# A transformer block on one core: x loaded a second time by tokens for its sums, warm-up matmuls, one power per norm, another order of projections

## The chip, the core and the metric

The kernel runs on one core of a Trainium2 chip. The metric is the device time of one execution in microseconds (us), lower is better. The engines named here are PE (the matrix engine, TensorE), PEld (its weight loads), DVE (VectorE), ACT (ScalarE), POOL (GpSimd) and SP, whose queue issues most transfers. Each engine runs its own instructions in the order in which the program holds them.

## What is computed

One block of a transformer on 512 tokens of width 1024 in fp32, cut here to its outline. Two attention mixers read the same normalized input, are gated and merged; a SwiGLU layer and a gated projection of a second input `p` follow.

```python
proj = rms_norm(x, g_mix) @ w_in                   # 1024 -> all heads, k, v, gates
q_n, kc_n, vc_n, ks_n, vs_n, kw_n, vw_n, gate_n, q_m, k_m, v_m, gate_a, gate_b = split(proj)
y_nsa  = nsa_mixer(...)    # 8 heads: compressed + selected + window attention, gated per head
y_moba = moba_mixer(...)   # 8 heads, causal, blocks of 256
x = x + (sigmoid(gate_a) * (y_nsa @ w_up_nsa) + sigmoid(gate_b) * (y_moba @ w_up_moba)) @ w_out
gate, up = split(rms_norm(x, g_ffn) @ w_ffn_in)    # 1024 -> 2 * 2816
x = x + (silu(gate) * up) @ w_ffn_out
x = x + sigmoid(rms_norm(x, g_ple) @ w_ple_gate) * (p @ w_ple_proj)
```

Queries and keys go through a norm over each head of 64 and a rotation of their first 16 elements (`partial_rope`) before the scores.

## The kernel before, in words

**Split numbers.** Every fp32 matrix is held as a high part (`wh`, `xh`) and a rest (`wl`, `xl`), and each product is three matmuls: high by high, high by rest, rest by high. A weight unit (128x1024, 512 KB) is loaded into one of three raw tiles `wr` on SP, copied to `wh` by ACT (line 83) and subtracted to `wl` by DVE (line 84). `Weights.units` lists the units in the order in which they are used; a unit is split about two units ahead of its matmuls, and each engine takes these copies in its own order among everything else.

**Start.** x comes transposed as eight tiles `xin` of 128x512. For each, ACT makes `xh` (line 220) and DVE `xl`; ACT squares it and POOL adds the squares up in `ssum` (lines 227 to 231). When the last is in, `rms_stats` sums `ssum` over partitions with four tiny matmuls into `st0b` (line 299) for the scales 1/rms of the 512 tokens; four more (`st0c`) spread the scales along rows.

**Projections.** `natural` multiplies a projection by four units of weights into four PSUM banks; the order is qm, km, qn (queries and keys of the two mixers), kT and vT with `compress_in` (inputs of the compressed keys and values), one gate tile, then cb and cc woven with the hidden layers of the compression (`khid`, `vhid`), then vm. `head_norm` squares on ACT, sums on DVE, takes the power -1/2 on POOL (line 356) for each 128-token tile, multiplies on DVE, rotates on POOL (lines 373 to 376) and splits on ACT and DVE (377, 378). `turned` transposes the result on PE into `QM`, `KM`, `QN`, `KN`.

**Attention.** 24 jobs, each of scores `sb` (711, 712), masks on DVE (714), exponentials on ACT (716), transposes `pt` of the probabilities (739), their split `pw` on ACT and DVE (748, 749) and products `pv` with the values. `weave` puts steps of other work between: `fill` (gate tiles `ga` and the projection `um`) at `FILL_RATE` steps per attention step, and `cmp_scores` at `CMP_RATE`. A scheduler then fixes each engine's order; the excerpts below are that order.

**Rest.** `un`, `wo`, the SwiGLU layer (`fi`, `fo`) and `pj`, `pg` follow, dense matmuls with weights streamed in.

Of the kernel before, what the change touches and what calls it, by code (L numbers as in the profile page):

```python
# [10 lines left out]
F32 = mybir.dt.float32  # L11
# [18 lines left out]
EARLY = 1  # L30
BIG_BUFS = 36
FILL_RATE = 0.83
CMP_RATE = 0.16
# [118 lines left out]
def hybrid_kernel(ctx: ExitStack, tc: tile.TileContext, a, out):  # L152
# [79 lines left out]

    for kt in range(KT):
# [62 lines left out]
    def rms_stats(name, tags="ss"):  # L296
        b = bank(name + "b", tags[0])
        for i in range(QT):
            T.matmul(b[:, i:i + 1], ssum[:, i * 128:(i + 1) * 128], ones[:, 0:1], start=True, stop=True)
        ms = small("ms_", [128, QT])  # L300
        V.tensor_scalar(ms, b[:, :QT], 1.0 / D, EPS, op0=OP.mult, op1=OP.add)
# [43 lines left out]
    def head_norm(items, nh, np_, gain, es, tables=None):  # L345
        n = nh * DH
        p = slice(0, np_)
        v3 = lambda t: t.rearrange("p (h d) -> p h d", d=DH)
        es = [e[p, :n] for e in es]
        for e, (src, ti, rn, r2, dst) in zip(es, items):  # L350
            A.activation(e, src, AF.Square)
            ss = small("ss_", [128, 8], bufs=4)
            V.tensor_reduce(ss[p, :nh], v3(e), axis=AX.X, op=OP.add)
            V.tensor_scalar(ss[p, :nh], ss[p, :nh], r2, EPS, op0=OP.mult, op1=OP.add)
            f = small("hf_", [128, 8], bufs=4)
            G.tensor_tensor(f[p, :nh], ss[p, :nh], half_neg[p, :nh], op=OP.pow)
            if rn is not None:
                V.tensor_scalar(f[p, :nh], f[p, :nh], rn, None, op0=OP.mult)
            V.tensor_tensor(v3(e), v3(src), f[p, :nh].unsqueeze(2).to_broadcast([np_, nh, DH]), op=OP.mult)

        def turn_and_split(k):
            e, (src, ti, rn, r2, dst) = es[k], items[k]
            e3 = v3(e)
            if gain is not None:
                V.tensor_tensor(e3, e3, gain[p].unsqueeze(1).to_broadcast([np_, nh, DH]), op=OP.mult)
            ct, st = tables or (cs2, sn2)
            w = t2("rope")[p]
            ra = w[:, 0:nh * 16].rearrange("p (h d) -> p h d", d=16)
            rc = w[:, 128:128 + nh * 16].rearrange("p (h d) -> p h d", d=16)
            cs = ct[p, ti].unsqueeze(1).to_broadcast([np_, nh, 16])  # L370
            s1 = st[p, ti, 0:8].unsqueeze(1).to_broadcast([np_, nh, 8])
            s2 = st[p, ti, 8:16].unsqueeze(1).to_broadcast([np_, nh, 8])
            G.tensor_tensor(ra, e3[:, :, 0:16], cs, op=OP.mult)
            G.tensor_tensor(rc[:, :, 0:8], e3[:, :, 8:16], s1, op=OP.mult)
            G.tensor_tensor(rc[:, :, 8:16], e3[:, :, 0:8], s2, op=OP.mult)
            G.tensor_tensor(e3[:, :, 0:16], ra, rc, op=OP.add)
            A.activation(dst[:, :, 0:DH], e3, AF.Copy)
            V.tensor_sub(dst[:, :, DH:128], e3, dst[:, :, 0:DH].bitcast(F32))

        return [lambda k=k: turn_and_split(k) for k in range(len(items))]  # L380
# [47 lines left out]
    def heads(sts, dst, tags, eng):  # L428
        for n in range(8):
            turned(sts, 2 * (n % 4), n // 4, tags[n % len(tags)], dst.tile(n % 4), eng)  # L430
            yield
# [8 lines left out]
    rb0, rn0, rhn0 = rms_stats("st0")  # L440
# [579 lines left out]
```

## Time and profile before

| what | value |
|---|---|
| time, median of 3 runs (all three) | 867.39 us (867.09, 867.39, 870.36) |
| the profiled execution | 869.85 us, its span 868.1 us |
| PE busy | 848.3 us, 98% of the span |
| DVE, ACT, POOL busy | 539.5, 388.2, 162.5 us |
| mean granted clock of TensorE | 0.991 |

The span runs from the first to the last instruction; the profiled execution has 1.75 us outside it. PE counts as busy from the start of a matmul to its modelled end, also when it runs at the lower clock, so 98% is not 98% of its peak. The granted clock is 1 at 2.4 GHz and 0.5 at 1.2 GHz.

### The profile page before, as it was taken

What the parts mean: (1) busy time and instruction counts of PE and PEld (TensorE: products, weight loads), DVE (VectorE), ACT (ScalarE), POOL (GpSimd) and SP (SyncE); (2) the same over time, 40 slices, a digit from 0 to 9 for tenths busy, and PEclk for the clock granted to TensorE, in tenths of its full rate; (3) what the DMA queues carried; (4) which work ended last, traced back from release to release, by engine and by line L of the source; (5) the groups of instructions that cost most, each with busy time, mean ns of one, the idle gap of its engine ahead of it and who ended that gap; (6) DMA issues with size and microseconds to landing.
All of it is one profiled execution on the core that took longest, in us unless ns stands there. A gap on an engine that the chain in (4) does not pass through costs nothing.

```text
span 868.1 us, 11091 instructions
## 1 busy us (share of the span) xinstructions
PE 848.3 (98%) x4157; PEld 710.9 (82%) x4157; DVE 539.5 (62%) x995; ACT 388.2 (45%) x702; POOL 162.5 (19%) x205
## 2 busy tenths in 40 slices
PE   7999999999999999999999999999999999999997
PEld 5787799788888888877888888888888888888886
DVE  7648967678997777749637555555555423333354
ACT  6344275677786677744433333333333223223421
POOL 6728914300000000006322111111111101010100
PEclk9999999999999999999999999999999999999999
DMA  7331365312311112115323223232323233333321
GB/s 249 102 98 61 90 186 183 99 49 73 98 49 50 52 48 70 33 67 189 124 75 97 98 97 97 98 98 97 97 97 97 85 94 106 91 109 97 97 97 48
DMA packets 26420, 83.49 MB, mean 96 GB/s; under 512 B 3328, under 2 KB 3840, under 8 KB 26368
## 3 DMA queue, kind: packets, MB, share of 16 engines
q1 hardware_dynamic: 25440, 80.69, 29.1%
q10 hardware_dynamic: 928, 2.11, 1.0%
q8 instruction: 32, 0.52, 0.2%
q14 instruction: 20, 0.16, 0.1%
HBM read 77.54 MB, written 2.10 MB: 92 GB/s over the span
## 4 chain that ended last, share of the span: by engine, by line
PE 86%; DVE 6%; POOL 3%; ACT 2%; issue 1%; DMA 1%; SPq 0%; ACTq 0%; POOLq 0%; DVEq 0%
PE fg L335 5%; PE fg L337 5%; PE fu L337 5%; PE fob L336 5%; PE fg L336 5%; PE fu L336 5%; PE fob L337 5%; PE fob L335 5%; PE fu L335 5%; PE ga L335 3%; PE ga L336 3%; PE ga L337 3%; PE pt L739 3%; PE pv L763 2%; PE pgb L335 2%; PE pgb L337 2%
## 5 line engine op out<-in xcount | busy, mean ns | idle before, releaser
L83 ACT ACTIVATE wh<-wr 128x1024 fp32r<-128x1024 f32 (+2 forms) x145 | 147.2, 1018 | 308.6 <-PE fu L336 69.8
L84 DVE TENSOR_TENSOR wl<-wr,wh 128x1024 fp32r<-128x1024 f32 (+2 forms) x145 | 195.2, 1348 | 112.9 <-ACT wh L83 111.6
L335 PE MATMUL fg<-x2h,wh 128*128 128x512 f32 x176 | 68.6, 390 | 0.0
L335 PE MATMUL fu<-x2h,wh 128*128 128x512 f32 x176 | 68.6, 390 | 0.0
L337 PE MATMUL fg<-x2h,wl 128*128 128x512 f32 x176 | 68.5, 389 | 0.0
L336 PE MATMUL fu<-x2l,wh 128*128 128x512 f32 x176 | 68.5, 389 | 0.0
L335 PE MATMUL fob<-HH,wh 128*128 128x512 f32 x176 | 68.5, 389 | 0.0
L336 PE MATMUL fg<-x2l,wh 128*128 128x512 f32 x176 | 68.5, 389 | 0.0
L337 PE MATMUL fob<-HH,wl 128*128 128x512 f32 x176 | 68.5, 389 | 0.0
L336 PE MATMUL fob<-HL,wh 128*128 128x512 f32 x176 | 68.5, 389 | 0.0
L337 PE MATMUL fu<-x2h,wl 128*128 128x512 f32 x176 | 68.5, 389 | 0.0
L908 POOL TENSOR_TENSOR u<-zg,u 128x512 f32<-128x512 f32 x22 | 29.9, 1360 | 199.7 <-DVE u L906 191.2
L231 POOL TENSOR_TENSOR ssum<-ssum,sqx 128x512 f32<-128x512 f32 x21 | 32.5, 1547 | 146.4 <-ACT sqx L230 146.3
L335 PE MATMUL ga<-xh,wh 128*128 128x512 f32 x128 | 53.5, 418 | 0.0
L714 DVE CUSTOM_DVE_ANT_0 p<-sb,big_mask 128x512 f32<-128x512 f32 (+2 forms) x96 | 44.4, 483 | 14.0 <-PE sb L712 13.8
L337 PE MATMUL ga<-xh,wl 128*128 128x512 f32 x128 | 51.2, 400 | 0.0
L336 PE MATMUL ga<-xl,wh 128*128 128x512 f32 x128 | 51.0, 398 | 0.0
L906 DVE SCALAR_TENSOR_TENSOR u<-fu,rb 128x512 f32<-128x512 f32 x22 | 15.2, 690 | 53.6 <-PE fu L337 53.6
L844 POOL TENSOR_TENSOR GT<-GT,GT 128x512 f32<-128x512 f32 x8 | 14.7, 1862 | 177.2 <-DVE GT L843 175.9
L336 PEld LDWEIGHTS fu<-x2l,wh 128*128 128x128 f32 x176 | 33.1, 188 | 6.9
L335 PEld LDWEIGHTS fob<-HH,wh 128*128 128x128 f32 x176 | 33.0, 188 | 6.9
L335 PEld LDWEIGHTS fg<-x2h,wh 128*128 128x128 f32 x176 | 33.1, 188 | 6.8
(640 smaller groups left out, 2028.3 us busy)
## 6 DMA issues: line engine op xcount, KB each, us to landing
wr<-fi SPq DMA_DIRECT2D x44, 512.0 KB, 3.3
wr<-ga SPq DMA_DIRECT2D x16, 512.0 KB, 3.5
wr<-fo SPq DMA_DIRECT2D x16, 512.0 KB, 3.5
wr<-wo SPq DMA_DIRECT2D x8, 512.0 KB, 3.4
wr<-pg SPq DMA_DIRECT2D x8, 512.0 KB, 3.3
wr<-fo SPq DMA_DIRECT2D x8, 384.0 KB, 3.1
xin<-xT SPq DMA_DIRECT2D x8, 256.0 KB, 5.8
wr<-km SPq DMA_DIRECT2D x4, 512.0 KB, 4.0
```

The source lines that it names most:

```text
L83: self.nc.scalar.activation(h[:, a:b], t[:, a:b], AF.Copy)
L84: self.nc.vector.tensor_sub(l[:, a:b], t[:, a:b], h[:, a:b].bitcast(F32))
L231: G.tensor_tensor(ssum, ssum, q, op=OP.add)
L335: T.matmul(o, wh[:, sl], h, start=start, stop=False)
L336: T.matmul(o, wh[:, sl], l, start=False, stop=False)
L337: T.matmul(o, wl[:, sl], h, start=False, stop=stop)
L714: V.tensor_tensor_reduce(out=p, in0=o, in1=big_mask[:, 512 - n:512], op0=OP.add, op1=OP.min, scale=1.0, scalar=3.0e38, accum_out=st["m"][: ...
L739: last = T.transpose(b[:, off:off + 128], st["p"][:, P_OFF[qt] + kb * 128:P_OFF[qt] + kb * 128 + 128], ident)
L763: T.matmul(o, job["v"](kb), st.pop(("pl", kb))[:, cols], start=False, stop=job["last"] and kb == 2)
L844: G.tensor_tensor(ta, ta, tb, op=OP.add)
L906: V.scalar_tensor_tensor(u, bu, 2.0, rb1, op0=OP.mult, op1=OP.mult)
L908: G.tensor_tensor(u, zg, u, op=OP.mult)
```

## The change

- The eight `xin` transfers stand ahead of everything else but the first weights; x comes a second time by tokens (`xN`, four tiles of 512 KB), and ACT squares these with a sum along each row (`sq`), in place of the squares, POOL's additions and the `st0b` matmuls.
- Eight fp32 matmuls of 128x128 on a tile of ones stand on PE ahead of the first real one.
- `head_norm` takes the power of all four tiles (128x32) in one POOL instruction, and sums, gains and rotations go by two tiles.
- kT and vT come right behind qm; `qn`'s transposes move behind cb; vm moves to just ahead of the attention; four steps of `fill`, the first score step and four more steps of `fill` come ahead of the weave; the compressed keys' chain (`cmp_kv`), `k_put` of cc and `cmp_scores` all run inside the attention at 0.28 steps per step; `FILL_RATE` 0.83 becomes 0.85.
- PSUM tags (`a`, `b`, `s`, `v`) are exchanged between cb, cc, khid, vhid and vm; `gsig` goes.

```diff
-FILL_RATE = 0.83
-CMP_RATE = 0.16
+WARM = 8
+FILL_RATE = 0.85
+CMP_RATE = 0.28
...
-    units = [*mixed("qm"), *mixed("km"), *mixed("qn")]
+    units = [*mixed("qm")]
     units += [(("kvc", i), a["kvc"][i], 1024) for i in range(2)]
+    units += [*mixed("km"), *mixed("qn")]
...
+    wb = bank("warm", "v")
+    for _ in range(WARM):
+        T.matmul(wb[:, 0:128], ones, ones, start=True, stop=True)
     for kt in range(KT):
         nc.sync.dma_start(xin[kt], a["xT"][kt])
-        if kt == 0:
-            W.load(1)
-        if kt % 2 == 1:
-            W.load(kt // 2 + 2)
+        if kt in (0, 3, 5):
+            W.load(W.n_raw + 1)
+    for kt in range(KT):
         norm_split(xin[kt], gv[:, 0, kt:kt + 1], xh[kt], xl[kt])
         if kt == 0:
             W.split(1)
-        add_square(xin[kt], kt == 0)
+    for tt in range(QT):
+        nc.sync.dma_start(flat(xn[tt]), a["xN"][tt])
+        A.activation(flat(xn[tt]), flat(xn[tt]), AF.Square, accum_out=sq[:, tt:tt + 1])
...
-        for e, (src, ti, rn, r2, dst) in zip(es, items):
-            A.activation(e, src, AF.Square)
-            V.tensor_reduce(ss[p, :nh], v3(e), axis=AX.X, op=OP.add)
-            G.tensor_tensor(f[p, :nh], ss[p, :nh], half_neg[p, :nh], op=OP.pow)
+        for g in groups:
+            for i in range(k, k + m):
+                A.activation(es[i], srcs[i], AF.Square)
+            V.tensor_reduce(ss[:, k * nh:(k + m) * nh], g[p].rearrange(...), axis=AX.X, op=OP.add)
+        G.tensor_tensor(f, ss, half_neg[p, :w], op=OP.pow)
...
-    cb_b = four("cb", "ab")
-    nat, hk = natural("cb", 256, cb_b), hidden("k", "s")
+    cb_b = four("cb", "sv")
+    nat, hk = natural("cb", 256, cb_b), hidden("k", "a")
...
-    side = k_put(kv_chunk(cb_b, 0, hg[:, 2]), 0, "b")
-    cc_b = four("cc", "vs")
-    nat, hv = natural("cc", 280, cc_b), hidden("v", "a")
+    side = chain(k_put(kv_chunk(cb_b, 0, hg[:, 2]), 0, "s"), heads(qn_t, QN, "s", "a"))
+    cc_b = four("cc", "ba")
+    nat, hv = natural("cc", 280, cc_b), hidden("v", "v")
...
-    cmp_side = cmp_scores()
-    fill = chain(gates(8 + EARLY, 16), up("um", YM, up_moba_done), gates(0, 8))
-    run(weave(weave(attention(jobs), fill, FILL_RATE), delay(cmp_side, 4), CMP_RATE))
+    vm_b = four("vm", "sv")
+    att = attention(jobs)
...
+    cmp_side = chain(cmp_kv(0, "k", "v"), cmp_kv(1, "v", "v"), side, cmp_scores())
+    fill = chain(gates(8 + EARLY, 16), gates(0, 2), up("um", YM, up_moba_done), gates(2, 8))
+    steps(fill, 4)
+    steps(att, 1)
+    steps(fill, 4)
+    run(weave(weave(att, fill, FILL_RATE), delay(cmp_side, 4), CMP_RATE))
```

**ACT's first work.** Behind two small loads ACT begins so before (`xh_86` is made from the first two tiles of x, `wh_90` from the first unit of weights, which comes in two halves):

```order
L227 ACTIVATE ssum<-xin_81 128x512
L220 ACTIVATE xh_86<-xin_81,gv 128x512
L83 ACTIVATE wh_90<-wr_83 128x512 x2
L220 ACTIVATE xh_86<-xin_81,gv 128x512
L230 ACTIVATE sqx<-xin_81 128x512
L83 ACTIVATE wh_190<-wr_98 128x1024
```

and so in the changed kernel, where `wh_115` is the first unit and `xh_111` the first two tiles:

```order
L84 ACTIVATE wh_115<-wr_94 128x512 x2
L223 ACTIVATE xh_111<-xin_92,gv 128x512 x2
L223 ACTIVATE xh_123<-xin_98,gv 128x512 x2
L84 ACTIVATE wh_186<-wr_101 128x1024
L223 ACTIVATE xh_129<-xin_103,gv 128x512
```

The first `xh` stood ahead of both halves of the first weights, and stands behind both now. PE's first real matmul needs it.

**PE where the attention starts.** Before, right behind the last matmuls of vm:

```order
L711 MATMUL sb<-KM_882,QM_528 128x512
L712 MATMUL sb<-k2M_1072,QM_528 128x512
L711 MATMUL sb<-KM_882,QM_528 128x384
L712 MATMUL sb<-k2M_1072,QM_528 128x384
L596 MATMUL kcT<-identr,MI 128x64
L392 MATMUL tb<-identr,kst 128x128 x4
L711 MATMUL sb<-KM_882,QM_528 128x256
L712 MATMUL sb<-k2M_1072,QM_528 128x256
L711 MATMUL sb<-KM_882,QM_528 128x128
L712 MATMUL sb<-k2M_1072,QM_528 128x128
L392 MATMUL tb<-identr,kst 128x128 x4
L711 MATMUL sb<-KM_882,QM_528 128x512
```

and in the changed kernel, behind eleven matmuls of the gate tile `ga` that follow vm:

```order
L733 MATMUL sb<-KM_899,QM_565 128x512
L734 MATMUL sb<-k2M_987,QM_565 128x512
L346 MATMUL ga<-xh_129,wh_1621 128x512
L347 MATMUL ga<-xl_130,wh_1621 128x512
L348 MATMUL ga<-xh_129,wl_1622 128x512
...
L348 MATMUL ga<-xh_135,wl_1622 128x512
L733 MATMUL sb<-KM_899,QM_565 128x384
L734 MATMUL sb<-k2M_987,QM_565 128x384
L733 MATMUL sb<-KM_899,QM_565 128x256
L734 MATMUL sb<-k2M_987,QM_565 128x256
L346 MATMUL ga<-xh_111,wh_1668 128x512
```

The transposes `tb` of the last keys left this place, and twelve gate matmuls stand between the first scores.

**PE where the attention ends.** Before, the transposes and products of the last two jobs have nine `uno` matmuls (the projection `un`) ahead of them and between:

```order
L763 MATMUL pv<-pw,VN_1080 128x512
L758 MATMUL pv<-pw,VN_1080 128x384
L335 MATMUL uno<-YNh_3134,wh_4145 128x512
...
L337 MATMUL uno<-YNh_3847,wl_4146 128x512
L763 MATMUL pv<-pw,VN_1080 128x384
L758 MATMUL pv<-pw,VN_1080 128x128
L763 MATMUL pv<-pw,VN_1080 128x128
L758 MATMUL pv<-phl,VN_1080 128x256
L763 MATMUL pv<-phl,VN_1080 128x256
L739 MATMUL pt<-ident,p 128x128 x8
L758 MATMUL pv<-pw,VN_1081 128x512
```

and in the changed kernel the last two jobs' transposes and products stand alone:

```order
L785 MATMUL pv<-phl,VN_996 128x256
L761 MATMUL pt<-ident,p 128x128 x4
L780 MATMUL pv<-pw,VN_995 128x512
L761 MATMUL pt<-ident,p 128x128 x2
L785 MATMUL pv<-pw,VN_995 128x512
L780 MATMUL pv<-pw,VN_995 128x384
...
L785 MATMUL pv<-phl,VN_995 128x256
L761 MATMUL pt<-ident,p 128x128 x4
L780 MATMUL pv<-pw,VN_996 128x512
L761 MATMUL pt<-ident,p 128x128 x2
L785 MATMUL pv<-pw,VN_996 128x512
```

Gate tiles and `uno` matmuls that stood here are used up some jobs earlier; one job more runs without other work between.

## Rows read from the trace of the kernel before

**Rows 1.** The page: each engine's busy time, share of the span, instructions.

```profile
PE 848.3 (98%) x4157; PEld 710.9 (82%) x4157; DVE 539.5 (62%) x995; ACT 388.2 (45%) x702; POOL 162.5 (19%) x205
```

**Rows 2.** PE's waits: instruction, releaser, total us, times, longest.

```profile
PE qm L325 <- ACT wh L83: 5.5, 1, 5.5
PE cb L326 <- DVE wl L84: 1.8, 1, 1.8
...
PE sb L711 <- DVE am__1912 L714: 1.3, 1, 1.3
PE st0b L299 <- POOL ssum L231: 1.3, 1, 1.3
PE cb L325 <- ACT wh L83: 1.3, 1, 1.3
```

**Rows 3.** Windows: stretch, its length, busy us by engine, PEclk, DMA.

```profile
30.00:35.00 5.00, 5.00 (x19) 4.17 (x20) 1.91 (x9) 1.07 (x2) 1.04 (x1) 0.66 0.00 1
...
110.00:115.00 5.00, 3.73 (x26) 3.54 (x25) 4.33 (x7) 4.97 (x8) 0.00 (x0) 0.74 0.43 119
...
170.00:175.00 5.00, 3.67 (x10) 2.83 (x10) 5.00 (x16) 4.79 (x17) 0.00 (x0) 0.56 0.34 107
175.00:180.00 5.00, 5.00 (x25) 4.22 (x24) 3.44 (x17) 2.64 (x9) 0.00 (x0) 0.75 0.00 0
...
240.00:265.00 25.00, 24.95 (x143) 21.23 (x142) 24.64 (x72) 21.38 (x49) 0.00 (x0) 1.00 0.15 45
```

**Rows 4.** Timeline of the start: start, us, engine, line, [idle before, releaser].

```profile
4.21 0.70 ACT L220 ACTIVATE xh<-xin,gv 128x512 fp32r<-128x512 f32 x1
...
4.83 0.63 ACT L83 ACTIVATE wh<-wr 128x512 fp32r<-128x512 f32 x1
...
5.51 2.08 PE L325 MATMUL qm<-wh,xh 128*128 128x512 f32 x4 [5.51 <-ACT wh L83]
...
7.25 0.63 ACT L83 ACTIVATE wh<-wr 128x512 fp32r<-128x512 f32 x1 [1.79 <-DMA wr<-qm]
...
10.39 0.39 PE L327 MATMUL qm<-wh,xl 128*128 128x512 f32 x1
```

**Rows 5.** PE's timeline around the sums of x.

```profile
29.90 1.18 PE L299 MATMUL st0b<-ones,ssum 128*128 128x1 f32 x8 [1.32 <-POOL ssum L231]
30.93 0.77 PE L325 MATMUL qm<-wh,xh 128*128 128x512 f32 x1
...
32.36 0.63 PE L326 MATMUL qm<-wl,xh 128*128 128x512 f32 x1
32.79 0.63 PE L327 MATMUL qm<-wh,xl 128*128 128x512 f32 x1
...
38.20 0.39 PE L326 MATMUL km<-wl,xh 128*128 128x512 f32 x1
38.43 0.39 PE L327 MATMUL km<-wh,xl 128*128 128x512 f32 x1
```

**Rows 6.** POOL's powers by form: count, busy, mean ns, idle before.

```profile
L356 POOL TENSOR_TENSOR hf__412<-ss__409,half_neg 128x8 f32<-128x8 f32 x1 | 1.6, 1631 | 0.0
...
L356 POOL TENSOR_TENSOR hf__1658<-ss__1655,half_neg 128x2 f32<-128x2 f32 x1 | 0.7, 696 | 0.0
```

**Rows 7.** ACT by form: the qn split, its idle time before, and the VC copies.

```profile
L377 ACT ACTIVATE qnst<-qne 128x512 fp32r<-128x512 f32 x4 | 2.5, 628 | 7.0 <-POOL qne L376 7.0
...
L607 ACT ACTIVATE VC<-MI 32x128 fp32r<-32x128 f32 x8 | 2.5, 309 | 0.4 <-DVE MI L604 0.3
```

**Rows 8.** PE's timeline in the last job of the attention.

```profile
379.24 1.06 PE L739 MATMUL pt<-ident,p 128*128 128x128 f32 x8
380.66 0.50 PE L758 MATMUL pv<-pw,VN 128*128 128x512 f32 x1 [0.36 <-ACT pw L748]
381.39 0.44 PE L739 MATMUL pt<-ident,p 128*128 128x128 f32 x2 [0.22 <-DVE pw L749]
...
382.44 0.45 PE L335 MATMUL uno<-YNh,wh 128*128 128x512 f32 x1
```

More of the change, by code (lines that the diff above doesn't have):

```diff
@@ L195, in hybrid_kernel @@
     units += [(("ga", i), a["ga"][i], 1024) for i in range(8 + EARLY, 16)]
+    units += [(("ga", i), a["ga"][i], 1024) for i in range(2)]
     units += [(("um", i), a["um"][i], 1024) for i in range(4)]
-    units += [(("ga", i), a["ga"][i], 1024) for i in range(8)]
+    units += [(("ga", i), a["ga"][i], 1024) for i in range(2, 8)]
     for nm, c in (("un", 4), ("wo", 8), ("fi", 44)):
@@ L241, in hybrid_kernel @@
             W.split(1)
-        add_square(xin[kt], kt == 0)
+    xn = [t4(f"xn{tt}", F32) for tt in range(QT)]
+    sq = cp.tile([128, QT], F32, name="sq")
+    for tt in range(QT):
+        nc.sync.dma_start(flat(xn[tt]), a["xN"][tt])
+        A.activation(flat(xn[tt]), flat(xn[tt]), AF.Square, accum_out=sq[:, tt:tt + 1])
     hg = cp.tile([128, 6, DH], F32, name="hg")
@@ L294, in rope_tables, with rms_stats @@
         G.tensor_scalar(sn2[:, :, 0:8], sn2[:, :, 8:16], -1.0, None, op0=OP.mult)
[L296 to L299, printed above, removed]
+    def rms_stats(name, tags="ss", sums=None):
+        if sums is None:
+            sums = bank(name + "b", tags[0])[:, :QT]
+            for i in range(QT):
+                T.matmul(sums[:, i:i + 1], ssum[:, i * 128:(i + 1) * 128], ones[:, 0:1], start=True, stop=True)
         ms = small("ms_", [128, QT])
-        V.tensor_scalar(ms, b[:, :QT], 1.0 / D, EPS, op0=OP.mult, op1=OP.add)
+        V.tensor_scalar(ms, sums, 1.0 / D, EPS, op0=OP.mult, op1=OP.add)
         rn = cp.tile([128, QT], F32, name=name + "rn")
@@ L375, in turn_and_split @@
[L375 to L380, printed above, removed]
+            ra = w[:, 0:m * nh * 16].rearrange("p (k h d) -> p k h d", k=m, d=16)
+            rc = w[:, 256:256 + m * nh * 16].rearrange("p (k h d) -> p k h d", k=m, d=16)
@@ L382, in s3 @@
+        t0 = tt0
+        rest = []
+        for g, dst in zip(groups, dsts):
+            rest.append(lambda g=g, t0=t0, dst=dst: turn_and_split(g, t0, dst))
+            t0 += g.shape[1]
+        return rest
     def s3(t, nh, p=128):
@@ L429, in heads @@
         for n in range(8):
[L430 removed]
+            turned(sts, 2 * (n % 4), n // 4, tags[n % len(tags)], dst.tile(n % 4), eng[n % len(eng)])
             yield
@@ L501, in gates @@
             A.activation(z, z, AF.Tanh)
-    run(weave(chain(compress_in(0, "k"), compress_in(1, "v"), gates(8, 8 + EARLY, "s")),
-              delay(chain(heads(km_t, KM, "vv", "v"), finish(rest)), 4)))
+    run(weave(chain(compress_in(0, "k"), compress_in(1, "v")), delay(finish(rest), 4)))
+    km_b = four("km", "sv")
+    run(weave(natural("km", 512, km_b), delay(heads(qm_t, QM, "a", "a"), 4)))
+    km_t, rest = norm_heads("km", km_b, hg[:, 5])
+    qn_b = four("qn", "ab")
+    run(weave(natural("qn", 512, qn_b), delay(finish(rest), 4)))
+    qn_t, rest = norm_heads("qn", qn_b, None, q_tables[0])
+    side = delay(chain(heads(km_t, KM, "v", "va"), finish(rest)), 2)
+    for _ in weave(gates(8, 8 + EARLY, "s"), side):
+        pass
     for i in range(2):
         swap(KM.tile(i), f"M{i}", nc.sync)
-    side = delay(heads(qn_t, QN, "v", "a"), 6)
+    side = chain()
     KN = [t4(f"KN{i}") for i in range(2)]
@@ L629, in hybrid_kernel @@
     side = k_put(kv_chunk(cc_b, 1, hg[:, 3]), 1, "v")
-    VMt = [[t4(f"VM{i}{k}") for k in range(2)] for i in range(2)]
-    VM = [[flat(VMt[i][k]).rearrange("p (k h d) -> p k h d", k=2, d=128) for k in range(2)] for i in range(2)]
-    vm_b = four("vm", "ab")
-    nat = natural("vm", 512, vm_b)
-    extra = delay(chain(weave(cmp_kv(0, "k", "v"), cmp_kv(1, "v", "s")), side), 4)
-    for n in range(16):
-        next(nat)
-        if n >= 12:
-            tt = n - 12
-            for i in range(2):
-                put_v(vm_b[tt][:, i * 256:(i + 1) * 256], rn0[:, tt:tt + 1], VM[i][tt // 2][:, tt % 2])
-        next(extra, None)
-    run(chain(nat, extra))
-    PC = [t4(f"PC{g}") for g in range(2)]
+    PC = {}
     def cmp_scores():
```

116 lines of the change are left out of this document (69 added, 47 removed).

## The prediction, made before the changed kernel ran

> **What bounds the kernel now.** The reader looks first at the shares of busy time: PE is busy for 98% of the span, every other engine for 62% or less [rows 1]. The work on PE hardly changes (4009 instructions before, 4007 after, by the two programs), so the change can only win or lose in the gaps of PE and in the stretches in which it runs at its lower clock. PE's waits come next [rows 2]: 5.5 us ahead of the first matmul, then 1.8 and 1.3 at cb, 1.3 at the second job's scores, 1.3 at `st0b`. They are short, but the windows show what they drag behind them: the granted clock is 0.66 in 30 to 35 us, 0.74 in 110 to 115, 0.56 and 0.75 in 170 to 180 [rows 3], each time behind one of these waits. A mean of 0.66 over 5 us is 0.34 x 5 = 1.7 us of full-rate work lost. So a wait of about 1.3 us costs some 3 us, and the places that the change touches before the SwiGLU layer hold some 20 us between them: the start, `st0b`, cb and the head of the attention. Behind the attention nothing is touched. The sum is made against the profiled execution, 869.85 us, which is 2.46 above the median of the three runs, 867.39; I carry the sum over to the median.
>
> **The first matmul.** Before, ACT makes `xh` at 4.21 and the first half of `wh` at 4.83, and PE starts at 5.51; the second half of `wh` waits for its transfer until 7.25 [rows 4]. Now both halves stand ahead of the first `xh`. The transfers that matter are issued in the same order at the start (x, both halves of the weights, x), so the second half should land when it did: ACT is free at 7.25 + 0.63 = 7.88, `xh` takes 0.70, PE starts at 8.58. That is **+3.1**. Bounds: +0.6 if both halves are there when x is (two copies of 0.63 and one of 0.70 from 4.2 on end at 6.1), +4 if it lands a microsecond later because two more tiles of x are in flight beside it. I take the row.
>
> **The warm-up matmuls.** They need only a tile of ones, so they lie in the empty time ahead. PE's first 4.9 us ran at the lower clock before (5.51 to 10.39, [rows 4]); at full rate half of that, 2.4 us, would be saved. The eight fp32 matmuls are sixteen records, two each like the four of `st0b` [rows 5]. Rows of 512 columns lie 0.43 apart at the lower clock [rows 5], which bounds the sixteen by 6.9 us from above and, by their 128 columns, 1.7 from below. From about 1.2 us on they end between 3 and 8; I take 4 to 5, which leaves a pause of some 4 us. The trace shows the clock down after waits of 1.3 and 1.8 us [rows 2, 3], so I take **0**; bounds 0 and -2.4.
> The Trainium skill (TensorE: Matmul & The Clock Gate, section "Loop structure matters more than you think") says that a PE which waits for a transfer drops to the lower clock. This trace agrees for other waits: 1.32 us at `st0b` were followed by 0.66. By that rule the warm-up is lost and the term is 0.
>
> **The sums of x.** Away go the wait of 1.32 us at `st0b`, its eight records (29.90 to 30.93, 1.03 us) and the stretch at the lower clock that follows, where starts lie 0.43 apart instead of 0.23 [rows 5], 1.7 us by its window [rows 3]: **-4.05**. In their place come 2 MB more on SP and four squares of 128x1024 on ACT. The transfers stand behind the weights of qm and one unit of kT, so nothing that PE needs before 30 us is queued behind them; by the scales' next user, `st0c` some 3 us after qm, the squares should be done. If the cover fails, PE waits there instead and the 1.3 + 1.7 come back: bounds -4.05 and -1.0.
>
> **Head norms.** Powers of 128x2 and 128x8 took 0.696 and 1.631 us [rows 6], 0.156 us for each further column, so 128x32 is estimated at 1.63 + 24 x 0.156 = 5.4 us. Four of 1.63 were 6.5. POOL gains 1.1 us for each norm, but the first tile's factor is 3.8 us later, and with it the multiplies, rotations and splits. For qm and km a whole projection lies ahead of the user: 0. For qn the splits on ACT already waited 7.0 us in all for POOL [rows 7]; now all four stand ahead of the weight copies of cb's third and later units, which PE needs.
>
> **cb and cc.** Against this, kT and vT have moved 50 us ahead, so `compress_in` no longer shares POOL and ACT with qn's rotations. What was lost around cb is 1.8 + 1.3 of waits [rows 2] and (1 - 0.74) x 5 = 1.3 of clock [rows 3], 4.4 in all. Behind cb come qn's transposes, the norm of two keys and cc's weights in one queue. I expect new waits of about the same sum: **0**, bounds -4.4 and +4.3.
>
> **The head of the attention.** Before, the second job's scores waited 1.33 us for DVE's masks, and the clock cost (1 - 0.56) x 5 = 2.2 and (1 - 0.75) x 5 = 1.25 [rows 2, 3]: 4.8. Now 23 gate matmuls (5.3 us at 0.23 [rows 5]) stand between vm and the first job's second score, more than the wait; the transposes of the last keys, which waited there too, have left. But DVE was busy for 5.00 of these 5 us [rows 3]: it still has the rest of vm ahead of the masks, so some of the wait stays without its clock. I leave 1.0 of it: **-3.8**, bounds -4.8 and 0.
>
> **Inside the attention.** The compressed keys' work now lies here; the VC copies alone are 2.5 us of ACT [rows 7], and DVE gets k_put's copies. DVE is at 24.64 of 25 in 240 to 265 [rows 3], so what falls there is paid: **+0.8**, bounds 0 and +3.
>
> **The end of the attention.** Eight steps of `fill` are spent ahead and the rate is higher, so the last but one job has no other work between its transposes and products. The last job, bare before, shows the price: from 379.24 to 382.44, 3.2 us [rows 8], in which ten transposes (1.06 for eight) and products of 2048 columns (four times 0.23) would take 2.0 or so: 1.2 us too long. One such job more: **+1.2**, bounds 0 and +2.4.
>
> **Sum.** 3.1 + 0 - 4.05 + 0 - 3.8 + 0.8 + 1.2 = -2.75, so 867.1 for the profiled execution and **864.6** at the median.
>
> **The rivals.** I call 0.5% (4.3 us: faster below 863.05, slower above 871.7) what can be told from no change.
> 1. *Cb and cc run clean.* The compressed inputs are ready 50 us early and PSUM tags no longer collide; all 4.4 goes: 864.6 - 4.4 = **860.2**, faster. For it: the longest wait there, 1.8 us, was for DVE's `wl` behind the very work that moves away. Against it: qn's splits, in front of weights.
> 2. *The warm-up holds the clock.* The weights' half lands early or the pause is too short for the clock to fall, and the 2.4 are saved: 864.6 - 2.4 = **862.2**. Against it: a pause of some 4 us, three times that at `st0b`. The Trainium skill (TensorE: Matmul & The Clock Gate, section "Why this matters for your kernels") advises to warm PE up with matmuls ahead of those that count; if that held across the pause, this would be the time.
> 3. *Qn's norm holds the weights (the other side).* If the 7.0 us that ACT waited for POOL [rows 7] now fall on PE, because the weight copies stand behind the splits, and the clock falls with it (1.7), while the old losses around cb stay, it is 864.6 + 8.7 = **873.3**, slower. It decides once the splits end more than 1.3 us after PE has used up the two units that are ready; for it speaks the later first factor, against it that POOL's load there is less by `compress_in`'s additions.
> 4. *The head of the attention gains nothing,* since DVE is full: 864.6 + 3.8 = **868.4**, same.
>
> **Chances.** Forecast 0.42, rival 1 0.25, rival 2 0.10, rival 3 0.10, rival 4 0.13. Of the forecast's own spread (861 to 868) a third lies below 863.05: faster 0.14 + 0.25 + 0.06 = 0.45; slower nearly all of rival 3, 0.09; same 0.46. The range leaves out rival 3 and joint luck below rival 1 with part of 2: 857 to 870.
>
> **What would show it.** PE's first real matmul at about 8.6 us behind an ACT copy that waits for a transfer; a granted clock of 1.00 in the windows from 30 to 35 us shifted by 3; no `st0b` wait; ACT idle before `qnst` for POOL, and whether PE's next wait is for `wh` there; the clock at the head of the attention near 1; two jobs at the end with waits of `pv` for `pw`. Wrong would make me: an early second half of the weights, a new wait in km or qn behind the 5.4 us power, or DVE paying more than 3 us between 180 and 260.

## The result, and the profile after

The changed kernel is slower: 876.45 us median of 7 runs (872.48 to 879.53) beside 867.39 (867.09 to 870.36, 7 runs with those shown), a ratio of 1.0095 with a 95% interval of 1.0070 to 1.0121. The forecast was 864.6, its range 857 to 870. The profiled execution took 878.48, its span is 876.8, 8.7 more than before.

PE's busy time grew by 4.7 us [rows 1], POOL's fell by 26.4, DVE's by 11.6; both had time to spare. The page after:

```profile
PE 853.0 (97%) x4165; PEld 713.4 (81%) x4165; DVE 527.9 (60%) x937; ACT 391.5 (45%) x700; POOL 136.1 (16%) x135
```

PE's waits after (instruction, releaser, total us, times, longest):

```profile
PE qm L336 <- ACT xh L223: 3.4, 1, 3.4
PE pt L761 <- DVE pw L771: 2.9, 6, 1.1
PE khid L581 <- ACT wh L84: 2.3, 1, 2.3
PE pv L780 <- ACT pw L770: 1.4, 2, 0.9
PE cb L336 <- ACT wh L84: 1.2, 1, 1.2
```

The waits for DVE's `am` at the second job and for `ssum` [rows 2] have left. New are `khid` for its weights, and the transposes and products of the attention, `pt` and `pv`, for the split probabilities `pw`. The windows after show where each lies:

```profile
30.00:35.00 5.00, 5.00 (x28) 4.29 (x27) 2.92 (x3) 2.48 (x4) 0.00 (x0) 1.00 0.34 105
112.00:117.00 5.00, 1.53 (x11) 1.12 (x9) 3.29 (x6) 3.26 (x6) 0.75 (x1) 1.00 1.03 219
117.00:122.00 5.00, 4.97 (x29) 4.94 (x29) 2.36 (x5) 1.88 (x5) 0.00 (x0) 0.66 0.93 241
166.00:171.00 5.00, 5.00 (x23) 4.13 (x23) 4.05 (x9) 2.99 (x6) 0.00 (x0) 1.00 0.30 112
171.00:176.00 5.00, 5.00 (x24) 3.67 (x22) 3.38 (x11) 3.56 (x9) 0.00 (x0) 1.00 0.29 105
220.00:240.00 20.00, 18.11 (x111) 15.50 (x110) 15.02 (x48) 15.56 (x41) 0.00 (x0) 1.00 0.27 79
240.00:265.00 25.00, 24.69 (x133) 21.21 (x133) 22.49 (x61) 15.50 (x35) 1.27 (x1) 0.93 0.14 44
265.00:280.00 15.00, 12.50 (x58) 9.73 (x55) 11.20 (x34) 9.63 (x25) 0.00 (x0) 0.89 0.11 35
```

The stretches from 30 and from 170 us, at 0.66 and 0.56 before [rows 3], run at full clock. PE does 1.53 us of work in the five from 112, the DMA engines are full there, and 0.66 follows. In 220 to 240 and 265 to 280 PE idles. In these two windows it did not idle at all before:

```profile
220.00:240.00 20.00, 20.00 (x118) 17.26 (x117) 18.59 (x55) 14.38 (x37) 0.00 (x0) 1.00 0.29 83
265.00:280.00 15.00, 15.00 (x85) 12.96 (x84) 10.71 (x29) 8.48 (x20) 0.00 (x0) 1.00 0.19 67
```

DVE, on which the forecast put the price there, is less busy after in the first (15.02 for 18.59) and hardly more in the second (11.20 for 10.71).

**PE's loss by stage.** To compare kernels by one measure, I worked out from each trace how much later each matmul on PE was followed by the next than in the median case of a matmul of that form in the kernel before, and added this up. It holds waits and the lower clock alike. The stages are cut at fixed times, so a kernel that is some us ahead shows part of cb's loss under 36 to 104. Each trace is one execution, and executions of one kernel differ: the 94 of the kernel before that were taken beside the experiments lasted 865.60 to 871.62 us, 18 of them with a mean granted clock of 0.998 (866.2 on average) and three with 0.989 (870.8); the one profiled took 869.85, at 0.991. In us:

| kernel | 0–36 | 36–104 | 104–145 | 145–220 | 220–350 | 350–410 | 410–end |
|---|---|---|---|---|---|---|---|
| before | 11.2 | 0.4 | 5.1 | 8.0 | 2.9 | 3.8 | 4.8 |
| after | 8.8 | 0.7 | 8.3 | 2.9 | 13.7 | 4.1 | 5.6 |

These sum to 36.2 and 44.1; with 0.8 more of work on PE (1.7 for the warm-up, less 0.9 for the records of `st0b`) that is the 8.7. The start loses 2.4 less and the head of the attention 5.1 less; cb and cc lose 3.2 more, and the inside of the attention 10.8 more. In this sum of two traces the last term alone turns the sign. What undoing it does to the time is another question (e8 below), and the start's 2.4 can't be told from how executions differ there (end of "The start").

### The profile page after: what moved, and what is told of

It is laid out like the page before. It is cut to its first block, busy times and chain, and to the rows that moved or that the text cites. A ratio compares the mean times of both kernels' runs of the same rounds, so it can differ in the third digit from the quotient of the medians.

```text
span 876.8 us, 10963 instructions
## 1 busy us (share of the span) xinstructions
PE 853.0 (97%) x4165; PEld 713.4 (81%) x4165; DVE 527.9 (60%) x937; ACT 391.5 (45%) x700; POOL 136.1 (16%) x135
## 4 chain that ended last, share of the span: by engine, by line
PE 88%; DVE 7%; ACT 3%; DMA 2%; issue 1%; SPq 0%; DVEq 0%; ACTq 0%
PE fg L346 5%; PE fu L347 5%; PE fg L347 5%; PE fob L346 5%; PE fu L346 5%; PE fob L348 5%; PE fg L348 5%; PE fob L347 5%; PE fu L348 5%; PE ga L346 3%; PE ga L348 3%; PE ga L347 3%; PE pt L761 3%; PE pgb L346 2%; PE pgb L348 2%; PE pgb L347 2%
## 5 line engine op out<-in xcount | busy, mean ns | idle before, releaser
L234 POOL TENSOR_TENSOR ssum<-ssum,sqx 128x512 f32<-128x512 f32 x14 | 22.1, 1578 | 139.1 <-ACT sqx L233 139.1
L761 PE MATMUL pt<-ident,p 128*128 128x128 f32 x240 | 39.0, 275 | 3.1 <-DVE pw L771 2.9
L771 DVE TENSOR_TENSOR pw<-pt,pw 128x512 fp32r<-128x512 f32 x48 | 32.4, 685 | 11.8 <-ACT pw L770 11.8
```

The costliest lines, as they stand in the source:

```text
L234: G.tensor_tensor(ssum, ssum, q, op=OP.add)
L761: last = T.transpose(b[:, off:off + 128], st["p"][:, P_OFF[qt] + kb * 128:P_OFF[qt] + kb * 128 + 128], ident)
L771: V.tensor_sub(pl, b[:, :off], ph.bitcast(F32))
```

## The experiments

Times are medians, in the order: kernel, kernel before on the same chip, ratio with its interval. "Loses" means the measure above.

### Which part of the change costs

Each part alone on the kernel before, and the attention's part alone taken out.

**e5_start_alone**: the warm-up, the order of loads and the sums by tokens.

> The kernel before with the start part alone: all of x transposed first, x by tokens for the sums, eight warm-up matmuls. By the terms of the prediction: first real matmul 1.5 to 3 us later, no wait and no low clock around the sums (-4.05), so 1 to 2.5 us below the kernel before, and everything behind 40 us as before but earlier. Rival: the longer queue of transfers delays later weights, and the gain is gone (within 1 us of before).

868.17 beside 867.66, 1.0014 (0.9992 to 1.0036): no gain that can be told. In the trace the start loses 7.5 instead of 11.2, and 145 to 220 loses 14.0 instead of 8.0. But that profiled execution took 874.31, 6.1 above the median of its kernel, so how much the others lose there isn't known; that a gain at the start is given back behind it is not shown by this run.

**e6_norm_alone**: the norm with one power (`gsig` dropped too).

> The kernel before with the batched head_norm alone (one power for four tiles, sums, gains and rotations by two; gsig dropped with it). If the single power of 5.4 us and what queues behind the qn splits is what costs 3 to 4 us around cb in the changed kernel: 870 to 872, the loss from 104 to 135 us 3 to 4 above before. If that loss comes from the order of projections or the PSUM tags: within 1 us of before.

868.32 beside 867.66, 1.0009 (0.9994 to 1.0023): no difference that can be told.

**e12_order_alone**: kT and vT behind qm, qn's transposes behind cb, tags and norm as before.

```diff
-    units = [*mixed("qm"), *mixed("km"), *mixed("qn")]
+    units = [*mixed("qm")]
     units += [(("kvc", i), a["kvc"][i], 1024) for i in range(2)]
+    units += [*mixed("km"), *mixed("qn")]
```

> The kernel before with the order of projections alone: kT and vT right behind qm, qn's transposes with cc. By subtraction of the runs so far (all but the attention part 5.8 above before, start 0.5, norm 0.7) this is worth 3 to 6 us: 870 to 873, lost around vm and at the head of the attention, where DVE and ACT have qn's transposes and the cc norm later than before. If the parts don't add up (the start's noise, the clock): within 1.5 of before, and cb and cc gain 2 to 3 us.

869.43 beside 867.20, 1.0027 (1.0011 to 1.0043). Its windows:

```profile
104.00:135.00 31.00, 30.46 (x245) 29.83 (x245) 24.11 (x51) 19.07 (x35) 9.74 (x21) 1.00 0.68 203
...
160.00:170.00 10.00, 8.08 (x37) 6.05 (x36) 7.72 (x26) 9.85 (x29) 0.76 (x4) 0.84 0.32 104
...
190.00:200.00 10.00, 8.27 (x41) 6.63 (x40) 7.45 (x19) 6.44 (x15) 0.00 (x0) 0.88 0.38 107
200.00:210.00 10.00, 9.78 (x45) 8.09 (x44) 4.28 (x11) 4.91 (x12) 0.00 (x0) 0.78 0.00 0
```

Cb and cc run clean, as rival 1 had it: PE busy for 30.46 of 31, full clock. But 145 to 220 then loses 13.6 instead of 8.0, in waits at 160 to 170 and 190 to 200 and the lower clock behind each. What the projections won, the first jobs of the attention took.

**e7_att_alone**: vm later, tags, the steps ahead, the compressed chain inside, the rates.

> The kernel before with the whole attention part alone: vm right ahead of the attention, gate matmuls ahead and between the first scores, compressed chain inside at 0.28, FILL_RATE 0.85, gates 0 and 1 ahead of umo, PSUM tags of cb, cc, hidden layers and vm exchanged. Theory A and B together (the attention part is where the 10.8 us between 220 and 350 us come from): the head gains 4 to 5, the stretch from 220 to 350 us loses 8 to 11 more, in all 871 to 876. If the stretch loses only as in the third run (4 more), the rest of the loss hangs on another part, and the time is 866 to 868.

873.42 beside 867.66, 1.0067 (1.0043 to 1.0091). 220 to 350 loses 11.9, 145 to 220 only 2.7.

**e8_att_undone**: the changed kernel with this part as before.

> The changed kernel with the whole attention part and the PSUM tags undone, so that start, batched head_norm and the order of projections stay. If the attention part holds the loss: 866 to 870, the stretch from 220 to 350 us back at 3 us, the head of the attention back at 7. If the order of projections or the norm disturb the attention: above 872.

873.50 beside 867.66, 1.0072 (1.0049 to 1.0095). 220 to 350 falls to 3.3 and 104 to 145 to 1.6, but 145 to 220 rises to 16.8. So taking out the part that holds the 10.8 brings the median only 3.0 below that of the changed kernel, with intervals that overlap, and not back to the kernel before as I expected.

The four parts alone add up to 0.5 + 0.7 + 2.2 + 5.8 = 9.2 us, the whole to 9.1. That the sum fits doesn't mean that the places do: each part moves its loss elsewhere than the whole does.

### The start

In the trace after, PE and ACT begin so (start, us, engine, line, [idle before, releaser]):

```profile
1.15 3.78 PE L240 MATMUL warm<-ones 128*128 128x128 f32 x16 [1.15 <-DVE half_neg L266]
...
7.02 0.63 ACT L84 ACTIVATE wh<-wr 128x512 fp32r<-128x512 f32 x1 [1.86 <-DMA wr<-qm]
...
7.55 2.55 ACT L223 ACTIVATE xh<-xin,gv 128x512 fp32r<-128x512 f32 x4
...
8.31 0.80 PE L336 MATMUL qm<-wh,xh 128*128 128x512 f32 x1 [3.38 <-ACT xh L223]
...
8.90 0.63 PE L337 MATMUL qm<-wl,xh 128*128 128x512 f32 x1
...
9.33 0.63 PE L336 MATMUL qm<-wh,xh 128*128 128x512 f32 x1
```

The warm-up ends at 4.93, `xh` waits behind the second half of the weights, and PE starts 2.8 us later than before [rows 4], its starts 0.43 apart, the spacing of the lower clock.

**e4_xh_first**: the changed kernel, the second half of the first weights held behind the first `xh`.

```diff
-                self.nc.scalar.activation(h[:, a:b], t[:, a:b], AF.Copy)
+                with (self.tc.issue_after(self.first) if a and i == 0 else nullcontext()):
+                    self.nc.scalar.activation(h[:, a:b], t[:, a:b], AF.Copy)
```

> The changed kernel with ACT's copy of the second half of the first weights held back behind the first xh. My reading of the start (that copy waits for its transfer and holds the first xh back): the first real matmul moves from 8.2 to about 5.5 us, 2.7 less, and the time to about 873.7. If instead the second half bounds the start anyway, because DVE's xl or the next matmuls wait for it: less than 1 us gained. If the warm-up holds the clock over the short pause that is then left, some 2 us more than the 2.7 are gained.

873.46 beside 868.79, 1.0062 (1.0039 to 1.0085): 3.0 us less than the changed kernel at the median, but the intervals of the two ratios overlap. PE's first matmuls there:

```profile
6.17 0.50 PE L339 MATMUL qm<-wh,xh 128*128 128x512 f32 x1 [1.29 <-ACT xh L224]
...
7.14 0.40 PE L339 MATMUL qm<-wh,xh 128*128 128x512 f32 x1
7.38 0.39 PE L340 MATMUL qm<-wl,xh 128*128 128x512 f32 x1
...
11.18 1.08 PE L340 MATMUL qm<-wl,xh 128*128 128x512 f32 x4
```

It starts at 6.17 and is soon at full rate, 0.24 apart. The start loses 5.8 instead of 8.8. Some of that is the arrival of the second half in the trace after: the other kernels with the start of the change begin between 6.70 and 8.72.

**e14_xh_first_no_warm**: the same without the warm-up matmuls.

> The fourth kernel (the changed one with xh first, 873.5) without the eight warm-up matmuls. If they hold the clock over the short pause that is left there (no low clock was seen in its profile): the first 4 to 5 us run at half the clock again, 1.5 to 2.5 us more, 875 to 876. If they do nothing: 873 to 874.

876.16 beside 867.09, 1.0086 (1.0052 to 1.0121). PE starts as early, at 6.01, and at the lower clock:

```profile
7.19 0.63 PE L338 MATMUL qm<-wh,xh 128*128 128x512 f32 x1
7.62 0.63 PE L339 MATMUL qm<-wl,xh 128*128 128x512 f32 x1
8.04 0.63 PE L338 MATMUL qm<-wh,xh 128*128 128x512 f32 x1
...
12.28 1.09 PE L339 MATMUL qm<-wl,xh 128*128 128x512 f32 x4
```

By the measure the start loses 8.7, 2.9 more than in e4, but the warm-up's own 1.7 us of work are gone too. In time, the same matmul, the seventeenth of `qm`, starts at 12.28 here and at 11.18 in e4. So the warm-up is worth 1.1 us where the pause behind it is 1.29 us. The intervals of the two ratios overlap; the starts are plainly spaced otherwise. The Trainium skill (TensorE: Matmul & The Clock Gate, section "Why this matters for your kernels") advises warming up with matmuls ahead of a measurement. This pair agrees with it, by 1.1 us. In the trace after nothing is won: its pause of 3.38 us is followed by the lower level.

**e13_start_xh_first** and **e16_sums_alone** carry the gain to the kernel before: the first with all of the start, the second with the sums by tokens alone, both with `xh` first.

> The kernel before with the start part alone, and with the copy of the second half of the first weights held behind the first xh. If the late first matmul was what ate the gain of the sums: 3 below the start part as it stands in the change (868.2), so 864 to 866 and below the kernel before. If the gain is given back later, at the head of the attention, whose order is planned anew: 867 to 869.

> The kernel before with the sums of x alone (x by tokens behind the other first loads, squares on ACT, no additions on POOL, no sums on PE), loads of x and weights in turn as before, no warm-up, xh first. The prediction's term: 4 us less, 863 to 864, no low clock at 30 to 35 us. If freeing POOL and ACT there only moves the stall to cb or to the head of the attention: 866 to 868.

866.91 and 866.58 beside 867.09: 0.9995 (0.9983 to 1.0007) and 0.9993 (0.9980 to 1.0006), no difference that can be told. The start loses 5.5 and 7.5 instead of 11.2, but 36 to 104 loses 2.9 in both instead of 0.4, 145 to 220 loses 9.5 in the first, and 410 to the end 0.8 more in both. The 2.9 is no price of the start: e6, e7, e10, e15 and e17, which leave the start as it was, lose 2.2 to 4.4 there. They are the fastest kernels of the study, and no faster than before.

**The start of the kernel before in other traces.** Seven kernels here leave the start as it was (e3, e6, e7, e10, e12, e15, e17). It loses 8.7 to 10.9 there, 8.7 to 9.0 in five of them, against 11.2 in the trace of before and 8.8 after. None of the seven runs the stretch from 30 to 35 us at the lower clock, as before did [rows 3]. In e3 the wait at `st0b` is longer than before's 1.32, and the clock stays up:

```profile
29.62 1.05 PE L299 MATMUL st0b<-ones,ssum 128*128 128x1 f32 x8 [1.66 <-POOL ssum L231]
...
30.00:35.00 5.00, 5.00 (x26) 4.21 (x27) 3.02 (x14) 2.14 (x3) 1.34 (x2) 1.00 0.00 0
```

So the low clock behind `st0b` is shown by the one execution that the forecast was read from, and by no other.

### Cb and cc

ACT, SP and PE after, where cb's third unit of weights is wanted:

```profile
111.19 2.19 ACT L407 ACTIVATE qnst<-qne 128x512 fp32r<-128x512 f32 x4 [2.67 <-POOL qne L402]
111.71 1.64 SPq L443 DMA_DIRECT2D k2M<-KM  x1
...
113.28 0.61 ACT L84 ACTIVATE wh<-wr 128x512 fp32r<-128x512 f32 x1
113.44 0.54 SPq L68 DMA_DIRECT2D wr<-cc  x1
...
113.95 0.74 PE L336 MATMUL cb<-wh,xh 128*128 128x256 f32 x4 [1.16 <-ACT wh L84]
...
115.92 1.06 ACT L84 ACTIVATE wh<-wr 128x1024 fp32r<-128x1024 f32 x1 [1.71 <-DMA wr<-k]
...
117.03 0.39 PE L581 MATMUL khid<-wh,kxx 128*128 128x256 f32 x1 [2.34 <-ACT wh L84]
```

This is rival 3's mechanism: the four `qnst` wait for POOL, the weights' copy stands behind them, PE waits for it. It is followed by a second wait that no rival named: ACT waits 1.71 us for `khid`'s weights, while the DMA engines are at 1.03 (the window from 112, above) and SP has issued the swaps `k2M` of km's keys just ahead.

**e18_old_tags**: the changed kernel with the tags of cb, khid, cc and vhid as before.

```diff
-    cb_b = four("cb", "sv")
+    cb_b = four("cb", "ab")
...
-    cc_b = four("cc", "ba")
+    cc_b = four("cc", "vs")
```

> The kernel after with the PSUM tags of cb, khid, cc and vhid as they were before (vm keeps its new tags). Theory A (the loss at cb and cc is made by the queue of ScalarE behind GpSimd's powers and by the DMA engines, not by the tags): 104 to 135 us still loses 7 to 9 us, and the time stays at 874 to 878. Rival B (the tags hold cb and cc back): 104 to 135 loses 2 to 4 us, and the time is 870 to 873.

882.11 beside 867.48, 1.0174 (1.0153 to 1.0195). The stretch and the time part ways. PE is busy for 29.67 of the 31 us from 104, as rival B had it, and then stands:

```profile
PE vm L336 <- DVE kve L386: 5.5, 1, 5.5
PE tb L427 <- ACT QN L434: 3.4, 3, 2.4
```

Vm takes the tags `s` and `v`, in which cc lies here, and has to wait until the norm of cc's keys has read it; 104 to 145 loses 12.8 instead of 8.3. So the exchange of tags frees vm, and the price for it was paid at cb. The tags alone don't make that price: from 36 to 145 us the changed kernel loses 9.0, e7 (new tags, old order and norm) 5.2, e8 (old tags, new order and norm) 3.2, and the kernel before 5.5. Why cb is later with the new tags, though PE's wait there is for weights, stays open. The scheduler places ACT's copies otherwise: in e18 weight copies go between the second and third `qnst` (108.09) and behind the fourth (110.08), in the changed kernel all four `qnst` stand together and the next weight copy starts at 113.28.

### Inside the attention

PE in the worst place of the trace after:

```profile
267.92 0.40 PE L348 MATMUL umo<-YMh,wl 128*128 128x512 f32 x1
...
270.76 0.66 PE L701 MATMUL pc<-ident,CD 128*128 128x128 f32 x4 [0.27 <-DVE PC L704]
...
273.17 0.51 PE L780 MATMUL pv<-pw,VN 128*128 128x512 f32 x1 [0.94 <-ACT pw L770]
274.74 0.44 PE L761 MATMUL pt<-ident,p 128*128 128x128 f32 x2 [1.06 <-DVE pw L771]
274.93 0.48 PE L785 MATMUL pv<-pw,VN 128*128 128x512 f32 x1
275.25 0.39 PE L346 MATMUL umo<-YMh,wh 128*128 128x512 f32 x1
```

Between two `umo` matmuls lie 7.3 us without any fill. What stands there is scores, transposes `pc` of the compressed scores, and products: work that itself waits for ACT and DVE. Behind it come twelve `umo` with a single product between, and the clock is low until 279.

**e2_fill83**: `FILL_RATE` back to 0.83 in the changed kernel.

> The changed kernel with FILL_RATE 0.83 instead of 0.85, nothing else. Theory A: within 2 us of the changed kernel, 874 to 878, since the compressed branch's steps stay where they are. Theory B: 869 to 872, and the waits for pw at 300 to 390 us become fewer.

877.57 beside 868.79, 1.0123 (1.0086 to 1.0159): the rate is not it. 220 to 350 loses 12.0.

**e1_cmp_ahead**: in the changed kernel the compressed chain goes back under vm, only `cmp_scores` stays inside, at 0.16.

> The changed kernel with one part undone: the compressed keys' chain (cmp_kv, k_put of cc) runs under vm as before, and cmp_scores alone lies inside the attention at 0.16 instead of 0.28. Theory A (the compressed branch's work on DVE and ACT, packed into 190 to 272 us, is what makes PE wait inside the attention): the loss of PE between 220 and 350 us, 13.7 us in the changed kernel and 2.9 before, falls to 3 to 5, the head of the attention loses 2 to 4 again, and the time comes to 868 to 870. Theory B (the gate and umo matmuls at 0.85 and the eight steps spent ahead are what starves PE of other work): within 2 us of the changed kernel.

873.69 beside 868.79, 1.0064 (1.0036 to 1.0091), not the 868 to 870 of theory A. 220 to 350 falls to 6.3, but 145 to 220 rises from 2.9 to 9.9: the first scores now wait 2.7 us for `VM`, behind DVE. The place of the chain and its rate change together here and in e3; no run changes `CMP_RATE` alone.

**e3_before_cmp_inside**: in the kernel before the chain goes inside, at 0.28.

```diff
-    cmp_side = cmp_scores()
+    cmp_side = chain(cmp_kv(0, "k", "v"), cmp_kv(1, "v", "v"), side, cmp_scores())
```

> The kernel before with this one part alone: cmp_kv, k_put of cc and cmp_scores in one chain inside the attention at 0.28 steps per step, nothing under vm. Theory A: the head of the attention loses less (its kcT and tb transposes leave, 1 to 3 us), the stretch from 220 to 350 us loses 8 to 11 more, in all 871 to 876. Theory B: 864 to 867.

869.20 beside 868.79, 1.0008 (0.9991 to 1.0025). 220 to 350 loses 6.9 (4.0 more), 145 to 220 loses 4.5 (3.5 less): an even trade. The chain inside is not enough.

**e9_no_scores**: the changed kernel without `cmp_scores`, which leaves out the scores of the compressed branch (`PC` is set to zero).

> The changed kernel without cmp_scores: the scores, softmax and transposes of the compressed branch are left out (PC is filled with zeros), cmp_kv and k_put stay inside the attention. Theory A: the stalls at 236 to 242 us (masks late, 2.0 us and the low clock behind) and at 268 to 280 (PC and pw late, 3.3 us and the low clock) go, the loss between 220 and 350 us falls from 13.7 to 4 to 6; some 7 to 9 us off, of which 1.5 are the work itself. Theory B (fill spent early and at another rate): the stalls stay, 2 to 3 us off.

867.23 beside 867.20, 0.9996 (0.9984 to 1.0009), 9.2 us below the changed kernel. PE has 4.3 us less work (I had put it at 1.5), and 220 to 350 loses 7.9 with no fall of the clock. So 5.8 of the 13.7 hang on `cmp_scores` and 5.0 over the 2.9 of before do not.

**e10_gates_ahead**: the kernel before with eight steps of `fill` ahead of the attention's weave, and two gates ahead of `um`.

> The kernel before with eight steps of fill spent ahead and around the first score step, and gates 0 and 1 ahead of umo; PSUM tags, compressed chain and rates as before. Theory B: 3 us or more lost between 220 and 350 us, 869 to 872. Theory A: that stretch stays at 3 us, the head of the attention gains or loses at most 2, 865 to 868.

869.61 beside 867.20, 1.0030 (1.0016 to 1.0044). 220 to 350 loses 4.3, 350 to 410 loses 6.0: the steps alone cost some 2 us, at the end more than inside.

**e11_no_steps**: the changed kernel without the eight steps.

> The changed kernel without the eight steps of fill ahead of the weave. If these gate matmuls are what freed the head of the attention (its banks s and v wait for vm's copies now): the head loses 3 to 6 us instead of 1.3 to 2, and the time is 878 to 882 if the rest stays; under theory B the stretch from 220 to 350 us gains 3 or more and the time is 873 to 877.

881.88 beside 867.20, 1.0169 (1.0135 to 1.0203). The first of the two expectations came true in part: 145 to 220 loses 5.4, 2.5 more than with the steps. The second did not: 220 to 350 loses 16.4, 2.7 more, where steps that cost would have given some back.

**e15_inside_and_steps** and **e17_inside_gates_first**: the kernel before with the chain inside, with and without the eight steps; both have two gates ahead of `um`, old tags and the rate 0.83.

```diff
+    att = attention(jobs)
+    steps(fill, 4)
+    steps(att, 1)
+    steps(fill, 4)
-    run(weave(weave(attention(jobs), fill, FILL_RATE), delay(cmp_side, 4), CMP_RATE))
+    run(weave(weave(att, fill, FILL_RATE), delay(cmp_side, 4), CMP_RATE))
```

> The kernel before with the compressed chain inside the attention (0.5 to 1 alone) and the eight steps of fill ahead with gates 0 and 1 ahead of umo (2.4 alone), PSUM tags and FILL_RATE as before. If the attention part's 5.8 come from these two together: 870 to 873, with the stalls at the jobs in which the compressed scores lie. If the exchanged tags hold the rest: 867 to 870.

> The kernel before with two edits: the compressed chain written inside the attention (as e3) and the first two gates written ahead of the product of the gates' weights, so that the fill hands them out first, without the eight early fill steps. Theory A (the eight steps ahead take work out of the fill that the compressed work needs beside it): the stretch 220 to 350 us loses about 7 us as in e3, and the time is 869 to 871. Rival B (the order of the fill alone, which filler lies beside the compressed work, makes the loss): 220 to 350 loses 12 to 14, and the time is 874 to 878.

With the steps 876.93 beside 867.09, 1.0110 (1.0077 to 1.0143); without them 869.01 beside 867.48, 1.0016 (1.0002 to 1.0030). The windows with the steps:

```profile
220.00:240.00 20.00, 16.29 (x91) 13.91 (x90) 14.00 (x39) 13.68 (x35) 0.00 (x0) 0.91 0.20 54
240.00:265.00 25.00, 24.52 (x144) 21.14 (x142) 24.08 (x64) 17.15 (x38) 0.74 (x1) 1.00 0.16 52
265.00:280.00 15.00, 13.12 (x62) 10.40 (x63) 9.83 (x30) 9.55 (x24) 0.00 (x0) 0.89 0.05 19
```

and without:

```profile
220.00:240.00 20.00, 18.76 (x108) 15.95 (x109) 18.43 (x51) 14.61 (x34) 0.73 (x1) 1.00 0.24 70
240.00:265.00 25.00, 23.62 (x134) 19.53 (x133) 23.79 (x67) 18.26 (x44) 0.00 (x0) 1.00 0.18 64
265.00:280.00 15.00, 15.00 (x86) 12.97 (x85) 10.73 (x31) 10.06 (x24) 0.00 (x0) 1.00 0.11 36
```

On the kernel before, the chain alone costs 0.4, the steps with the gates' order 2.4, the chain with the gates' order 1.5, and chain and steps together 9.8, with the same 13.7 lost in 220 to 350 as after the whole change. Tags, start, norm and order of projections are not needed for it.

## Why the prediction was wrong, step by step

- **The step that failed is "Inside the attention: +0.8, bounds 0 and +3".** It measured 10.8. It lies far outside what executions differ by: 220 to 350 loses 11.9 to 13.9 in the six traces with the attention as changed (after, e2, e4, e7, e14, e18) and 2.5 to 3.3 in the seven with the attention as before (before, e5, e6, e8, e12, e13, e16). I priced the compressed keys' work by the busy time that it adds to DVE at 240 to 265 [rows 3]. DVE was less busy there after (22.49 of 25). What the rows show instead is PE waiting in stretches of the chain from scores to products in which no fill stands: stretches without a single fill matmul reach 7.3 us after, 8.7 in e15 and 7.5 in e11, and 3.9 at most between 180 and 375 before. The length alone doesn't set the loss: e3 has one of 6.8 and e17 two, of 6.4 and 6.3, at about half the loss or less (6.9 and 5.3). That the missing fill is the cause, and that fill in those places would mend it, is argued from the rows and wasn't tried.
- **Where fill goes is decided by the scheduler from the whole program, and I took it from the code's order.** I costed the steps ahead at the two ends of the attention only (-3.8 and +1.2). On the kernel before they cost 8.3 together with the chain inside (9.8 in e15 less 1.5 in e17) and 2.4 without it; on the changed kernel taking them out costs 5.4 (e11). No one edit is the cause there, and what rule of the scheduler sets it stays open.
- **Cb and cc: 0, bounds -4.4 and +4.3.** It measured +3.2 between the two traces. By all traces it is nearer to +2: from 36 to 145 us the eight that leave this part as it was (before, e3, e5, e10, e13, e15, e16, e17) lose 5.5 to 8.1, 6.3 on average, and the seven that have it whole as changed (after, e1, e2, e4, e9, e11, e14) 6.8 to 9.0, 8.2 on average. I let the old losses and the new ones cancel; rival 1 is what the order does alone (e12), rival 3's queue is what it does with the rest, and the DMA engines, full at that place, add a wait. The 5.4 us of the power was right, as this group of POOL's by form shows:

```profile
L382 POOL TENSOR_TENSOR hf__708<-ss__701,half_neg 128x32 f32<-128x32 f32 x1 | 5.4, 5436 | 14.9 <-DVE ss__701 L381 14.9
```

- **First matmul: right.** Start at 8.31, forecast 8.58, for the reason given; that it came so close is luck, since the same issues gave 6.70 to 8.72 in other kernels. **Warm-up: right** in this kernel, though in e4 it pays 1.1, under half of rival 2's 2.4.
- **Sums of x: -4.05, put too high.** The wait at `st0b`, its records and its low clock are gone. But the 1.7 of clock was in no other trace that leaves this part as it was, and the wait itself runs there from nothing (e10) to 1.66 (e3). With the 1.03 of the records the change is worth about 1.0 to 2.7 by these traces. First matmul, sums and warm-up together were put at -0.95; beside the trace of before the start's loss fell by 2.4, less 0.8 of added work: -1.6, of which nothing is sure, since 8.8 lies within the 8.7 to 10.9 of an unchanged start.
- **One execution was taken for the kernel.** The sum takes off stretches of low clock that the execution of 869.85 us had, and was then carried over whole to the median, 867.39. If the median execution lacks the clock behind `st0b`, as those seven traces do, up to 1.7 us was taken off twice. That a wait of about 1.3 us costs some 3 holds for this trace and not as a price: the 1.66 of e3 cost no clock.
- **Head norms: 0, right** as a sum (e6).
- **Head of the attention: right.** -3.8 forecast, 5.1 less lost in 145 to 220, full clock in 166 to 176. But e8 and e12, which win ahead of it, lose 16.8 and 13.6 in that stretch: there gains are given back. E5 loses 14.0 in an execution far above its median. With the attention's part whole (after, e2, e4, e7) it loses 2.7 to 3.4.
- **End of the attention: smaller than put.** +1.2 forecast, 0.3 more lost in 350 to 410.

Without the failed term's excess of 10.0 and cb's 3.2 the profiled span would have been shorter than before by 4.5, where the forecast was -2.75; 1.6 of the 4.5 is the start, which isn't sure. The list of places was good in the main, the one that I had called nearly free was not.

## What to carry to other kernels

By the account argued above, work that is put beside a chain of dependent steps on PE is filler only if it doesn't itself wait for the same engines: count the matmuls in each stretch that depend on nothing recent, not the busy share of the engine that gets more. Where a scheduler orders the engines, price two edits together as well as apart, and don't count on a gain early in the program until the next place with little slack has kept it (e12). Before a stretch of low clock is priced, see whether other executions have it too. ACT takes its copies in order, so they should stand in the order in which their inputs land: holding one copy back behind the first `xh` brought PE's first matmul from 8.31 to 6.17.

## What the runs showed of the hardware that was not expected

- The second half of the first weights, behind the same issues, let PE start at 6.70 (e1), 7.54 (e18), 8.31 (after) and 8.72 (e9): about 2 us of chance in the arrival, which moves the whole program.
- The clock after the warm-up differed with little in the pause: 1.76 us was followed by starts 0.43 apart in e1, 1.82 us by 0.23 in e11. The column PEclk reads 1.00 at the start of both, so there the spacing has to be read.
- Nor did equal waits at `st0b` have equal effect: 1.32 us in the trace of before was followed by a granted clock of 0.66 in 30 to 35 us, 1.33 in e12 and 1.66 in e3 by 1.00.
